# Last super-block: new keys and values turned by VectorE and a way through DRAM, undivided last jobs, and a last row scaled by two engines

## The chip, the cores and the metric

The kernel runs on one core of a Trainium2 chip. The metric is the device time of one execution in microseconds. The core has TensorE (PE in the profile; its weight loads are PEld), VectorE (DVE), ScalarE (ACT), GpSimd (POOL) and SyncE (SP), which issues nearly all DMAs of this kernel. TensorE writes into eight PSUM banks; the other data lies in SBUF or in DRAM.

## The reference

One layer of a streaming encoder. 2048 prompt rows and 64 rows of a running stream, 1024 wide, are normalised and multiplied by one input matrix of 4096 columns. Half of the columns feed attention (8 heads of 64), half a gated linear recurrence (4 heads of 128). Cut to what matters here:

```python
def mixer_layer(x, ln_g, w_in, lb, norm_g, w_out, attn_fn, s0):
    aq, ak, av, ag, hq, hf, hi, hg = jnp.split(rms_norm(x, ln_g) @ w_in, SPLITS, axis=-1)
    k, v = heads(ak), heads(av)
    o_a = attn_fn(heads(aq), k, v).reshape(B, T, W_A) * jax.nn.silu(ag)
    o_b, S = hgrn2_branch(hq, hf, hi, hg, lb, norm_g, s0)
    y = x + jnp.concatenate([o_a, o_b], axis=-1) @ w_out
    return y, k, v, S

# attention: each chunk of 64 frames sees itself and the 8 chunks before it, plus a learned bias
# recurrence, per block of frames (b: running sum of log f, bl: its last value):
S = jnp.exp(bl)[..., None] * S + jnp.einsum('bshk,bshv->bhkv', kb * jnp.exp(bl[:, None] - b), vb)
# outputs: final RMSNorm of y for prompt and sample, the last 512 rows of k and v of the prompt
# and the 64 of the sample, and the recurrent states
```

The rows of k and v that are returned for the prompt are the last 512, which are exactly the rows of the last super-block below. `kb * exp(bl - b)` are the decayed keys.

## The kernel before, in words

**Tiling.** The rows are worked in four super-blocks: rows 0 to 511, rows 512 to 1023 with the 64 sample rows (576), rows 1024 to 1535, rows 1536 to 2047. In each, 32 jobs (`project`) multiply the normalised input, held transposed with features on partitions, by 128 columns of the input matrix. Every float32 operand is split into a high and a low part, so one job is 24 matmuls of 128x128 weights over 512 columns, or over 256 and 320 in the 576-row super-block. Jobs have a kind and a number: `hf hq hi hg` for the heads 0 to 3 of the recurrence, `pg pq pk pv` (gate, query, key, value) for the pairs 0 to 3 of attention heads. The result lands transposed in a PSUM bank `acc` (two of them): features on partitions, rows of the sequence along the free axis.

**After a job.** Each kind has a function that empties the bank (`ev_f`, `ev_k`, ...). Some data must be turned, so that sequence rows lie on partitions:
- values: for the super-blocks 0 to 2, `ev_v` lets DVE transpose 32x32 blocks out of `acc` (`turn_blocks`), sends them to a DRAM room with four DMAs, and fetches them back with one (`turn_rows`), after which whole rows of 128 features stand on the partitions. For the last super-block, `ev_v_last` copies the bank to a tile `vT`, turns it by eight 64x64 TensorE transposes for the product with V, and by four 128x128 ones for the rows to be returned (`new_rows`: transposes into bank `tr`, DVE copy to a tile `sig` at L645, one DMA).
- keys: `ev_k` copies the bank to `vT`, splits it into the key tile `kd`, and in the last super-block `new_rows` turns and returns the rows.
- input values of the recurrence (`ev_i`): the DVE and DRAM way in every super-block.
- decayed keys (`rec_block`): tile `kh` (buffer `bl`), per 128 rows one TensorE transpose into a bank `g` and an ACT copy to `kn` (L1474), which is then the weight operand of the product with the input values.

The silu gates and the forget gates (`silu_to` at L575, `ev_f` at L1248) also pass through `sig`, of which there are two buffers; `vT` has three. `ev_k` copies at L794, `ev_v_last` at L815.

**Jobs in halves.** The second job and the last two of a super-block are run in two halves of 256 columns, so that the two halves of the rows can be taken over one after the other between super-blocks; this includes the last two jobs of the last super-block, `pk` and `pg` of pair 3.

**The end.** The output projection runs as 7 products of 12 matmuls for each of 8 row pairs (`out_step`), added to the residual (`out_add`); POOL adds in two pieces of 256. `out_norm` is called for each half of a row tile (128 rows x 512 columns): ACT squares and sums it; after the second half ACT makes the inverse root, and DVE scales by it and the gain vector `g_in` (L1860), half after half, each with a DMA by SP.

**What sets the order.** The program order of every engine is written out at build time by a planner (`Plan`): generators yield the time from which they can go on, tokens (`tk`) stand for buffers and banks, and `C.dve`, `C.act`, `C.dma` advance a modelled clock of each engine and of SP's queue. On the chip each engine and SP's queue then run strictly in that order, with semaphores between them. TensorE's order interleaves jobs with attention, recurrence and output steps. Weight loads (L446) wait on SP for TensorE to free one of four weight buffers.

Of the kernel before, what the change touches and what calls it, by code (L numbers as in the profile page):

```python
# [8 lines left out]
F32 = mybir.dt.float32  # L9
# [3 lines left out]
ALU = mybir.AluOpType  # L13
# [4 lines left out]
P = 128  # L18
# [165 lines left out]
def hymba_step(  # L184
# [439 lines left out]
    def new_rows(src, off, bn, p, out_p, out_s, tok, t):  # L624
# [29 lines left out]
            tk["sig"].put()  # L654
        tk["tr"].put(1, t)

    def split_rows(src, v, h, t0, nt, rows, t):
        s = src.rearrange("p (h a t j) -> p h a t j", h=2, a=2, t=nt)[:, h]
        hi, lo = (v[:rows, h, t0 : t0 + nt, x, :].rearrange("p t (a j) -> p a t j", a=2) for x in (h, 1 - h))
        act.copy(hi, s)  # L660
        t = C.act(nt * 64 + 80, t)
        yield "D", t
        dve.tensor_sub(lo, s, f32(hi))
        return C.dve(nt * 64 + 30, t)
# [74 lines left out]
    def pair_jobs(sb, p):  # L739
        t0, n = SUPER[sb][:2]  # L740
        last = sb == len(SUPER) - 1
        smp = n > WIN
        d = Pair()
        d.sb, d.p = sb, p
# [45 lines left out]
        def ev_k(acc, off, bn, t):  # L790
            yield from tk["vT"].get()
            yield "A", t
            kn = T(wk, [P, 512], F32, "vT", bufs=VTB)
            act.copy(kn[:, :bn], acc)  # L794
            t = C.act(bn, t)
            tk["acc"].put(1, t)
            c = slice(512 + off, 512 + off + bn)
            for h in range(2):
                yield lambda: d.open[h]
                yield "A", t  # L800
                act.copy(d.kd[own[h], h, c], kn[own[h], :bn])
                t = C.act(bn, t)
                yield "D", t
                dve.tensor_sub(d.kd[own[1 - h], h, c], kn[own[h], :bn], f32(d.kd[own[h], h, c]))
                t = C.dve(1.2 * bn, t)
                d.k_n[h] += bn
                d.k_t[h] = max(d.k_t[h], t)
            yield from new_rows(kn, off, bn, p, nk_prompt if last else None, nk_sample, tk["vT"], t)
            yield from got_all(True)

        def ev_v_last(acc, off, bn, t):
# [28 lines left out]
        def ev_v(acc, off, bn, t):  # L840
            yield from tk["vT"].get()
            yield "D", t
            vt = T(wk, [P, 512], F32, "vT", bufs=VTB)
            t = turn_blocks(vt, acc, bn)
            tk["acc"].put(1, t)
            t = yield from turn_rows(vt, bn, t)
            full = bn // P * P
            parts = [p_ for p_ in ((0, full, P, None),
                                   (full, P if bn > full else 0, bn - full, nv_sample)) if p_[1]]
            for c, w, rows, out in parts:  # L850
                if out is not None:
                    rows_out(vt[:rows, c : c + w], out, slice(p * P, (p + 1) * P), t)
            for h in range(2):
                yield lambda: d.open[h]
                for c, w, rows, _ in parts:
                    yield "A", t
                    t = yield from split_rows(vt[:rows, c : c + w], d.v, h, 4 + (off + c) // P, w // P, rows, t)
                d.v_n[h] += bn
                d.v_t[h] = max(d.v_t[h], t + 500.0)
            tk["vT"].put(1, t)  # L860
            yield from got_all(False)

        def all_in():
# [37 lines left out]
            yield from gate(acc, off, bn, t)  # L901
            d.sg_n += bn

        return d, dict(g=ev_g, q=ev_q, k=ev_k, v=ev_v_last if last else ev_v)

    def softmax_rows(d, h, qc, spans, bcol, nk, out):

# [428 lines left out]
    def rec_block(r, off, bn, lastb):  # L1336
# [10 lines left out]
        def v3(t):  # L1347
            return t[:, :bn].rearrange("p (b t) -> p b t", t=32)
# [86 lines left out]
                              fk[:, :nprc].unsqueeze(3).to_broadcast([P, nprc, 2, 32]), ALU.mult)  # L1435
            td = C.dve(1.9 * bn, td)
        qh, kh = tmp("bm"), tmp("bl")
        dve.tensor_tensor(v3(kh), v3(k1), sf[:, :nb].unsqueeze(2).to_broadcast([P, nb, 32]), ALU.mult)
        tkh = C.dve(1.3 * bn)
        dve.tensor_tensor(v3(qh), v3(q1), pf[:, :nb].unsqueeze(2).to_broadcast([P, nb, 32]), ALU.mult)  # L1440
        tqh = C.dve(1.3 * bn)

# [19 lines left out]
            m = mask[:w, :w].unsqueeze(1).to_broadcast([w, cs.stop - cs.start, w])  # L1462
            dve.copy_predicated(A[:w, cs, :w], m, ag[:w, cs, :w])
        ta = C.dve(1.1 * bn, t)
        yield max(ta, tkh) + 200.0
        tg = bank()
        for i, (cc, nbk, smp) in enumerate(chunks):
            w = nbk * 32
            transpose(tg[:w, i], kh[:, cc : cc + w], ident)
        t = C.pe()  # L1470
        yield "A", t
        kn = tmp("k1").rearrange("p (c t) -> p c t", t=P)
        for cs, w in merged():
            act.copy(kn[:w, cs], tg[:w, cs])  # L1474
        t = C.act(bn, t)
        yield t + 200.0
        kv = bank()
        iv = r.iv
        for i, (cc, nbk, smp) in enumerate(chunks):
# [343 lines left out]
    def out_norm(o, tile_, half, t):  # L1823

        rows = o["rows"]
        x = o["res"][tile_]
        end = o is outp.get(len(pairs) - 1)
        yield "A", t
        yield from tk["ck"].get()
        junk = T(wk, [P, D], mybir.dt.bfloat16, "ck", bufs=1)  # L1830
        ss = T(wk, [P, 1], F32, "ss", bufs=4)
        act.activation(junk[:rows, :512], x[half][:rows], AF.Square, accum_out=ss[:rows])  # L1832
        t = C.act(800, t)
        tk["ck"].put()
        if tile_ not in o["first"]:
            o["first"].add(tile_)
            b0 = T(wk, [P, 1], F32, "b0", bufs=4)
            yield "D", t
            dve.tensor_scalar(b0[:rows], ss[:rows], 1.0 / D, EPS, ALU.mult, ALU.add)
            C.dve(10, t)  # L1840
            o["b0"][tile_] = b0
            return
        yield lambda: tile_ in o["b0"]
        r = T(wk, [P, 1], F32, "rstd", bufs=4)
        act.activation(r[:rows], ss[:rows], AF.Ln, bias=o["b0"][tile_][:rows], scale=1.0 / D)
        act.activation(r[:rows], r[:rows], AF.Exp, scale=-0.5)
        t = C.act(400, t)
        y = o["y"][tile_]
        if x[3] is not None and not end:
            yield "D", t  # L1850
            dve.scalar_tensor_tensor(x[3][:rows], x[3][:rows], r[:rows], g_in[:rows], ALU.mult, ALU.mult)
            t = C.dve(1070, t)
            yield t
            sp.dma_start(y, x[3][:rows])
            C.dma(512 * rows / P)
        else:
            for a in range(2):
                c = slice(a * 512, a * 512 + 512)
                yield "D", t
                dve.scalar_tensor_tensor(x[a][:rows], x[a][:rows], r[:rows], g_in[:rows, c], ALU.mult, ALU.mult)  # L1860
                t = C.dve(530, t)
                yield t
                sp.dma_start(y[:, c], x[a][:rows])
                C.dma(256 * rows / P)
        for tag in x[2]:
            tk[tag].put(1, C.now + 4000.0)
# [46 lines left out]
    def program():  # L1913
# [66 lines left out]
        for sb in range(nsb):  # L1980
            last = sb == nsb - 1
            halves = SUPER[sb][3]
            blocks = SUPER[sb][2]
            if sb == 2:
                C.spawn(out_weights(), 3)
            made = {}
            for u, (kind, g) in enumerate(JOBS[sb]):
                if u == len(JOBS[sb]) - 8:
                    if last:
                        C.spawn(out_load(0), 1.5)  # L1990
                        C.spawn(out_load(1), 1.6)
                        for rows in (out_rows_w(), out_rows_g(), out_rows_x(), out_rows_a()):
                            C.spawn(rows, 2)
                    else:
                        for half in range(2):
                            off, bn = SUPER[sb + 1][3][half]
                            for c in range(off, off + bn, P):
                                C.spawn(x_tile(sb + 1, half, c), 0.5 + 0.1 * half)
                if (kind[0], g) not in made:
                    d, evs = made[kind[0], g] = (head_jobs if kind[0] == "h" else pair_jobs)(sb, g)  # L2000
                    C.spawn((recurrence if kind[0] == "h" else attention)(d), 1)
                evac = made[kind[0], g][1][kind[1]]

                if u in (1, len(JOBS[sb]) - 1):
                    for half in range(2):
                        yield from project(j - 1, [halves[half]], before, half == 1,
                                           lambda part, k0: x_ready(sb, half, part, k0))
                        yield from project(j, [halves[half]], evac, half == 1,
                                           lambda part, k0: x_ready(sb, half, part, k0))
                        if u > 1:  # L2010
                            x_left[sb, half] = True
                elif u not in (0, len(JOBS[sb]) - 2):
                    yield from project(j, blocks, evac)
                before = evac
                j += 1
        for i, k in steps:
# [147 lines left out]
```

## Time and profile before

| what | value |
|---|---|
| median of 3 runs | 1251.13 us (1250.59 to 1251.42) |
| profiled execution | 1251.06 us |
| its span, first to last instruction | 1249.3 us, granted clock 0.998 |
| TensorE busy | 1237.7 us, 7520 matmuls |
| DVE, ACT, POOL busy | 886.6, 684.4, 412.3 us |
| DMA | 287.94 MB in 137956 packets, 230 GB/s |

The span lies within the profiled execution's time; 1.8 us are outside it. A row of TensorE is a matmul from its start to its modelled end, and the next one starts before that end, so lengths of rows don't add up, while the distances from start to start do. The last super-block's jobs run from about 805 to 1065 us; the output steps follow until 1242.7 us, and the last row's work until the end.

### The profile page before, as it was taken

Reading aid. Unit: us, or ns where it says so; the run is one execution under the profiler, and the core shown is the slowest. Engines: PE = TensorE matmul, PEld = TensorE weight load, DVE = VectorE, ACT = ScalarE, POOL = GpSimd, SP = SyncE. Lnnn points to the kernel's source line nnn. Section 1 sums busy time; section 2 is a strip of 40 time slices with the busy share of each in tenths; the row PEclk is TensorE's granted clock in tenths of the full one; section 3 lists DMA queues with packets and bytes.
Section 4 is the critical chain, followed back from the end, with each engine's and each line's share of the span. In section 5 each row is a group of like instructions: output and inputs, shape, how many; then the busy total and the mean of one; then the engine's idle time right before and its main releaser. Section 6 shows DMA issues by size and latency. Waiting matters only on the chain. (4 is left out here: it accounts for less than half of the span.)

```text
span 1249.3 us, 21363 instructions
## 1 busy us (share of the span) xinstructions
PE 1237.7 (99%) x7520; PEld 1088.6 (87%) x7520; DVE 886.6 (71%) x1889; ACT 684.4 (55%) x1534; POOL 412.3 (33%) x702
## 2 busy tenths in 40 slices
PE   9999999999999999999999999999999999999997
PEld 8888888999999999998888888988888888788786
DVE  7697878866767578776576677775757476767775
ACT  6354545665656556574555566664655445643443
POOL 7666564101020111200233242133241103474543
PEclk9999999999999999999999999999999999999999
DMA  8897888666565474654777778687766655887431
GB/s 337 301 325 257 313 301 318 203 192 222 166 195 166 144 276 155 206 178 150 284 247 252 266 263 280 227 258 248 231 243 210 218 203 211 333 273 237 139 123 68
DMA packets 137956, 287.94 MB, mean 230 GB/s; under 512 B 35257, under 2 KB 79289, under 8 KB 120186
## 3 DMA queue, kind: packets, MB, share of 16 engines
q1 hardware_dynamic: 137560, 286.58, 67.6%
q8 instruction: 59, 0.97, 0.3%
q14 instruction: 47, 0.39, 0.1%
q10 hardware_dynamic: 290, 0.01, 0.0%
HBM read 195.31 MB, written 92.27 MB: 230 GB/s over the span
## 5 line engine op out<-in xcount | busy, mean ns | idle before, releaser
L249 PE MATMUL acc<-xh,w 128*128 128x512 f32 (+2 forms) x2752 | 568.6, 345 | 0.5 <-ACT xh L409 0.5
L249 PEld LDWEIGHTS acc<-xh,w 128*128 128x128 f32 x2752 | 439.3, 189 | 50.6 <-ACT xh L409 0.9
L249 PE MATMUL acc<-xl,w 128*128 128x512 f32 (+2 forms) x1376 | 294.8, 345 | 0.0
L249 PEld LDWEIGHTS acc<-xl,w 128*128 128x128 f32 x1376 | 221.1, 189 | 24.4
L939 ACT ACTIVATE pr<-pr,nm 128x640 f32<-128x640 f32 (+4 forms) x132 | 100.4, 761 | 60.0 <-DVE nm L922 59.5
L951 ACT CAST ph<-tr 128x512 fp32r<-128x512 f32 (+3 forms) x176 | 88.2, 507 | 78.5 <-PE pv L249 45.8
L922 DVE CUSTOM_DVE_ANT_0 pr<-s,bias 128x640 f32<-128x640 f32 (+4 forms) x128 | 94.2, 736 | 41.1 <-PE s L249 40.3
L473 POOL TENSOR_TENSOR w<-wraw,w 128x256 fp32r<-128x256 f32 x120 | 102.4, 884 | 55.0 <-DVE w L468 43.1
L954 DVE TENSOR_TENSOR ph<-tr,ph 128x512 fp32r<-128x512 f32 (+3 forms) x176 | 101.2, 588 | 26.3 <-ACT ph L951 25.5
L249 PE MATMUL pv<-ph,v 128*128 128x256 f32 (+2 forms) x344 | 98.6, 370 | 0.1
L253 PE MATMUL tr<-ident,pr 128*128 128x128 f32 x580 | 88.1, 273 | 1.3 <-DVE ph L954 1.3
L993 DVE TENSOR_TENSOR mixa<-mixa,pv 64x256 f32<-64x256 f32 (+1 forms) x144 | 56.9, 395 | 43.3 <-ACT mixa L989 39.7
L510 POOL TENSOR_TENSOR xn<-wraw,xn 128x256 fp32r<-128x256 f32 x48 | 39.0, 814 | 142.4 <-ACT xn L507 137.1
L1095 POOL TENSOR_TENSOR mixa<-mixa,sga 128x256 f32<-128x256 f32 (+1 forms) x36 | 27.9, 776 | 162.8 <-DVE mixa L993 152.0
L253 PEld LDWEIGHTS tr<-ident,pr 128*128 128x128 f32 x580 | 69.7, 140 | 10.9 <-issue 1.7
L943 DVE TENSOR_SCALAR pr<-pr,sm 128x640 f32<-128x640 f32 (+4 forms) x132 | 74.6, 565 | 4.7
L1532 POOL TENSOR_TENSOR k<-ob 128x512 f32<-128x512 f32 (+2 forms) x20 | 18.2, 910 | 176.0 <-ACT ob L1523 136.0
L575 ACT ACTIVATE sig<-acc 128x512 f32<-128x512 f32 (+2 forms) x64 | 32.2, 503 | 74.6 <-PE acc L249 72.0
L249 PEld LDWEIGHTS pv<-ph,v 128*128 128x128 f32 (+1 forms) x344 | 58.2, 189 | 7.3 <-issue 0.5
L989 ACT COPY mixa<-pv 64x256 f32<-64x256 f32 (+1 forms) x72 | 25.2, 350 | 64.8 <-PE pv L249 59.5
L249 PE MATMUL s<-kd,q 128*128 128x320 f32 (+2 forms) x232 | 55.8, 310 | 0.0
L249 PE MATMUL s<-kd,ql 128*128 128x320 f32 (+2 forms) x232 | 55.5, 309 | 0.0
(333 smaller groups left out, 2133.3 us busy)
## 6 DMA issues: line engine op xcount, KB each, us to landing
w<-wd SPq DMA_DIRECT2D x96, 1024.0 KB, 5.8
wd<-w SPq DMA_DIRECT2D x32, 1024.0 KB, 7.3
wraw<-in_w_in_dram SPq DMA_DIRECT2D x30, 512.0 KB, 5.3
wod<-xn SPq DMA_DIRECT2D x28, 512.0 KB, 5.5
xn<-in_x_prompt_dram SPq DMA_DIRECT2D x23, 512.0 KB, 4.6
bias<-biasd SPq DMA_DIRECT2D x24, 320.0 KB, 5.9
carry<-kd SPq DMA_DIRECT2D x12, 512.0 KB, 7.0
carry<-v SPq DMA_DIRECT2D x12, 512.0 KB, 5.5
```

What stands on the lines that cost most here:

```text
L249: pe.matmul(out, w, x, **kw)
L253: pe.transpose(out, x, idn)
L473: pool.tensor_sub(w[:, 1, k : k + 2], raw[:, k : k + 2], f32(w[:, 0, k : k + 2]))
L510: pool.tensor_sub(f32r(st[:, c.start + 512 : c.stop + 512]), src[:, c], st[:, c])
L575: act.activation(sig[:, :bn], acc, AF.Exp, scale=-1.0)
L922: dve.tensor_tensor_reduce(s[:, :nk].rearrange("p (a c) -> p a c", a=ns), sps[:, :ns, :kn], d.bias[:, h, bcol : bcol + nk].rearrange("p (a ...
L939: act.activation(s[:, :nk], s[:, :nk], AF.Exp, bias=nm[:, 0:1], scale=-1.0, accum_out=sm)
L943: dve.tensor_scalar(s[:, :nk], s[:, :nk], sm, None, ALU.mult)
L951: act.copy(ph[:krows, 0, :wid], pt[:krows, :wid])
L954: dve.tensor_sub(ph[:krows, 1, :wid], pt[:krows, :wid], f32(ph[:krows, 0, :wid]))
L993: dve.tensor_add(mix[hs, :qn], mix[hs, :qn], pv[hs, i, :qn])
L1095: pool.tensor_mul(mix[:, :n], mix[:, :n], d.sg[:, g0 : g0 + n])
```

## The change

- Keys of pairs 0 to 2 in the last super-block: the rows to be returned are turned by `turn_blocks` into a `sig` tile and a way through DRAM (`block_rows`), and go out by four DMAs with pieces of 128 bytes (`rows_to`). Pair 3 keeps the transposes.
- Values of the same pairs: `ev_v`, the way of the other super-blocks, takes the place of `ev_v_last`; the rows go out by `rows_to`, and the `vT` tile is kept 4 us longer in the planner's time.
- Decayed keys of heads 0 and 1 in super-blocks 1 to 3: written in the order that the way needs, turned by DVE, sent through DRAM beside the rest of the block, and copied by ACT from SBUF instead of from PSUM.
- The last two jobs of the last super-block run whole, one after the other.
- The last row tile: the half that is finished first is multiplied by the gain on DVE while the other is still summed; at the end ACT scales it and issues its DMA, and DVE scales the other half, which SP sends.

```diff
+    def rows_to(src, out, off, w, p):
+        s4 = src.rearrange("q (a t j) -> q t a j", a=4, j=32)
+        for i in range(w // P):
+            row = off + i * P
+            sp.dma_start(out[row : row + P, p * P : (p + 1) * P].rearrange("q (a j) -> q a j", a=4), s4[:, i])
+            C.dma(64)
+            yield C.now + 800.0
+
+    def block_rows(src, off, bn, p, out, tok, t):
+        yield from tk["sig"].get()
+        yield "D", t
+        st = T(wk, [P, 512], F32, "sig", bufs=2)
+        t = turn_blocks(st, src, bn)
+        tok.put(1, t)
+        t = yield from turn_rows(st, bn, t)
+        yield t
+        yield from rows_to(st[:, :bn], out, off, bn, p)
+        tk["sig"].put(1, C.now + 4000.0)
...
+        by_blocks = last and p < NPAIR - 1
...
+            if by_blocks:
+                yield from block_rows(kn, off, bn, p, nk_prompt, tk["vT"], t)
+            else:
+                yield from new_rows(kn, off, bn, p, nk_prompt if last else None, nk_sample, tk["vT"], t)
...
+                elif by_blocks:
+                    C.spawn(rows_to(vt[:, c : c + w], nv_prompt, off + c, w, p), 2)
...
-            tk["vT"].put(1, t)
+            tk["vT"].put(1, t + (4000.0 if by_blocks else 0.0))
...
-        return d, dict(g=ev_g, q=ev_q, k=ev_k, v=ev_v_last if last else ev_v)
+        return d, dict(g=ev_g, q=ev_q, k=ev_k, v=ev_v_last if last and not by_blocks else ev_v)
...
+        by_dma = sb > 0 and h < 2
...
+                dve.tensor_tensor(kh4, k14, sf[:, : 4 * nprc].rearrange("p (c b) -> p c b", b=4).unsqueeze(3)
+                                  .to_broadcast([P, nprc, 4, 32]), ALU.mult)
...
+                    dve.transpose(kh[:, a_[0] : a_[1]], kh[:, a_[0] : a_[1]])
...
+                rows["t"] = yield from turn_rows(kh, bn, tkh)
...
+            yield lambda: "t" in rows
+            yield rows["t"]
+            kn = tmp("k1").rearrange("p (c t) -> p c t", t=P)
+            if nprc:
+                act.copy(kn[:, :nprc].rearrange("p c (a j) -> p c a j", j=32),
+                         kh[:, :full].rearrange("p (a c j) -> p c a j", a=4, j=32))
...
+            if end and tile_:
+                yield "D", 0.0
+                c = slice(half * 512, half * 512 + 512)
+                dve.tensor_mul(x[half], x[half], g_in[:, c])
+                C.dve(530)
+                o["scaled"] = half
...
+        elif end and tile_:
+            a = o["scaled"]
+            act.mul(x[a], x[a], r)
+            act.dma_start(y[:, a * 512 : a * 512 + 512], x[a])
+            c = slice((1 - a) * 512, (1 - a) * 512 + 512)
+            dve.scalar_tensor_tensor(x[1 - a], x[1 - a], r, g_in[:, c], ALU.mult, ALU.mult)
+            sp.dma_start(y[:, c], x[1 - a])
...
-                if u in (1, len(JOBS[sb]) - 1):
+                if u == 1 or (u == len(JOBS[sb]) - 1 and not last):
...
-                elif u not in (0, len(JOBS[sb]) - 2):
+                elif u != 0 and (last or u != len(JOBS[sb]) - 2):
                     yield from project(j, blocks, evac)
+                    if u == len(JOBS[sb]) - 1:
+                        x_left[sb, 0] = x_left[sb, 1] = True
```

More of the change, by code (lines that the diff above doesn't have):

```diff
@@ L807, in ev_k @@
                 d.k_t[h] = max(d.k_t[h], t)
-            yield from new_rows(kn, off, bn, p, nk_prompt if last else None, nk_sample, tk["vT"], t)
+            if by_blocks:
+                yield from block_rows(kn, off, bn, p, nk_prompt, tk["vT"], t)
+            else:
+                yield from new_rows(kn, off, bn, p, nk_prompt if last else None, nk_sample, tk["vT"], t)
             yield from got_all(True)
@@ L1437, in rec_block, with row_way @@
         qh, kh = tmp("bm"), tmp("bl")
-        dve.tensor_tensor(v3(kh), v3(k1), sf[:, :nb].unsqueeze(2).to_broadcast([P, nb, 32]), ALU.mult)
-        tkh = C.dve(1.3 * bn)
+        by_dma = sb > 0 and h < 2
+        full = nprc * P
+        rows = {}
+        if not by_dma:
+            dve.tensor_tensor(v3(kh), v3(k1), sf[:, :nb].unsqueeze(2).to_broadcast([P, nb, 32]), ALU.mult)
+            tkh = C.dve(1.3 * bn)
+        else:
+            if nprc:
+                k14, kh4 = (a_[:, :full].rearrange(o_, b=4, j=32) for a_, o_ in
+                            ((k1, "p (c b j) -> p c b j"), (kh, "p (b c j) -> p c b j")))
+                dve.tensor_tensor(kh4, k14, sf[:, : 4 * nprc].rearrange("p (c b) -> p c b", b=4).unsqueeze(3)
+                                  .to_broadcast([P, nprc, 4, 32]), ALU.mult)
+            if bn > full:
+                k13, kh3 = (a_[:, full:bn].rearrange("p (b j) -> p b j", j=32) for a_ in (k1, kh))
+                dve.tensor_tensor(kh3, k13, sf[:, 4 * nprc : nb].unsqueeze(2).to_broadcast([P, nb - 4 * nprc, 32]),
+                                  ALU.mult)
+            C.dve(1.3 * bn)
+            for a_ in ((0, full), (full, bn)):
+                if a_[0] < a_[1]:
+                    dve.transpose(kh[:, a_[0] : a_[1]], kh[:, a_[0] : a_[1]])
+            tkh = C.dve(1.1 * bn)
+            def row_way():
+                rows["t"] = yield from turn_rows(kh, bn, tkh)
+            C.spawn(row_way(), 1)
         dve.tensor_tensor(v3(qh), v3(q1), pf[:, :nb].unsqueeze(2).to_broadcast([P, nb, 32]), ALU.mult)
@@ L1464, in rec_block @@
         ta = C.dve(1.1 * bn, t)
[L1465 to L1476, printed above, removed]
+        kn = None
+        if by_dma:
+            yield ta + 200.0
+            yield lambda: "t" in rows
+            yield rows["t"]
+            kn = tmp("k1").rearrange("p (c t) -> p c t", t=P)
+            if nprc:
+                act.copy(kn[:, :nprc].rearrange("p c (a j) -> p c a j", j=32),
+                         kh[:, :full].rearrange("p (a c j) -> p c a j", a=4, j=32))
+            if bn > full:
+                act.copy(kn[:DEC, nprc], kh[:DEC, full : full + P])
+            t = C.act(bn, rows["t"])
+            yield t + 200.0
+        else:
+            yield max(ta, tkh) + 200.0
+            tg = bank()
+            for i, (cc, nbk, smp) in enumerate(chunks):
+                w = nbk * 32
+                transpose(tg[:w, i], kh[:, cc : cc + w], ident)
+            t = C.pe()
+            yield "A", t
+            kn = tmp("k1").rearrange("p (c t) -> p c t", t=P)
+            for cs, w in merged():
+                act.copy(kn[:w, cs], tg[:w, cs])
+            t = C.act(bn, t)
+            yield t + 200.0
         kv = bank()
```

## The prediction

> **What bounds the kernel now.** I read the page first for busy shares, then the list of what TensorE waits for, then TensorE in order of time around the instructions that go, and last the end of the chain.
>
> ```profile
> span 1249.3 us, 21363 instructions
> PE 1237.7 (99%) x7520; PEld 1088.6 (87%) x7520; DVE 886.6 (71%) x1889; ACT 684.4 (55%) x1534; POOL 412.3 (33%) x702
> ...
> PE tr L253 <- DVE ph L954: 1.3, 1, 1.3
> PE acc L249 <- DVE pr L1783: 0.6, 1, 0.6
> ```
>
> TensorE is busy 99% of the span, and its longest wait after the start is 1.3 us. Busy alone could hide waits, because a matmul's row lasts longer than the time to the next one, so I use the distance between starts:
>
> ```profile
> 863.39 1.99 PE L249 MATMUL acc<-xh,w 128*128 128x512 f32 x8
> 865.22 0.60 PE L253 MATMUL tr<-ident,vT 128*128 128x128 f32 x4
> 865.58 0.70 PE L249 MATMUL acc<-xh,w 128*128 128x512 f32 x2
> 866.12 0.45 PE L249 MATMUL s<-kd,q 128*128 128x320 f32 x2
> ...
> 867.25 0.46 PE L253 MATMUL tr<-ident,vT 64*128 64x64 f32 x4
> 867.65 1.20 PE L249 MATMUL acc<-xh,w 128*128 128x512 f32 x4
> 868.68 0.62 PE L249 MATMUL acc<-xl,w 128*128 128x512 f32 x2
> ...
> 912.06 0.60 PE L253 MATMUL g<-ident,bl 128*128 128x128 f32 x4
> 912.41 0.72 PE L249 MATMUL acc<-xl,w 128*128 128x512 f32 x2
> 912.97 0.62 PE L249 MATMUL pv<-ph,v 128*128 128x512 f32 x2
> ```
>
> Columns: start, length, engine, line, tiles, shape, count. Eight 512-wide matmuls take 863.39 to 865.22, 0.229 us each, with no hole when the transposes come between. So TensorE is a full queue: the time is the sum of what it is given, plus the last row after it. An instruction taken off it is worth its distance to the next start, if what it made still comes in time from elsewhere.
>
> **Transposes taken off TensorE.** A group's price is from its start to the second row behind it, less the matmuls between at 0.229, because a group's last transpose shows its cost only in the matmul behind it.
> - Four 128x128 transposes for output rows: 866.12 - 865.22 - 2 x 0.229 = 0.44 us. Keys and values of pairs 0 to 2: 6 groups, 2.6 us.
> - Four 64x64 transposes that bring one head's values into place: 868.68 - 867.25 - 4 x 0.229 = 0.51 us. Two heads, three pairs: 6 groups, 3.1 us.
> - Decayed keys: 912.97 - 912.06 - 2 x 0.229 = 0.45 us for four, 0.112 each.
>
> ```profile
> L253 PE MATMUL g<-ident,bl 128*128 128x128 f32 x64 | 10.2, 272 | 0.0
> ...
> L253 PE MATMUL g<-ident,bl 128*64 128x128 f32 x4 | 1.1, 272 | 0.0
> ```
>
> 64 and 4 are those of four heads, so 17 a head. A head has four of the wide ones in super-block 0, where nothing changes; 13 stay to be removed for each of heads 0 and 1: 26 x 0.112 = 2.9 us. The three together: 8.6 us.
>
> **What takes their place.** On DVE the rows of keys were a copy of 512 columns from PSUM and become a 32x32-block transpose of 512; the values' row copy likewise gives way to one block transpose; only the decayed keys gain an instruction, eight of at most 0.71 us, some 6 us over 950 us. ACT loses three copies of values (L815).
>
> ```profile
> L671 DVE STREAM_TRANSPOSE vT<-acc 128x512 f32<-128x512 f32 x18 | 12.8, 711 | 5.3 <-PE acc L249 5.2
> ...
> L645 DVE COPY sig<-tr 128x512 f32<-128x512 f32 x7 | 4.8, 690 | 3.7 <-PE tr L253 3.7
> ...
> 900.00:950.00 50.00, 50.00 (x292) 42.27 (x292) 31.67 (x65) 28.17 (x59) 18.27 (x26) 1.00 0.72 249
> ```
>
> In that stretch of the last super-block DVE is busy 31.7 of 50 us, so it covers this at no cost; without the cover it would be at most those 6 us. The clock granted is 1.00 and DMA engines are busy 0.72, also with room.
>
> SP's queue gets more. A way is four DMAs out and one back; rows are four DMAs instead of one. Keys or values of a pair: +8, six times 48; heads 0 and 1: five parts a head (1, 2, 1, 1 over the blocks), five DMAs each, +50. At 0.43 us an issue 98 DMAs are 42 us, 24 us of them (58 DMAs) in the last super-block.
>
> ```profile
> SPq L446 <- PE acc L249: 94.5, 23, 12.0
> ...
> SPq L695 <- DMA way<-vT: 9.2, 5, 5.6
> ...
> L691 SPq DMA_DIRECT2D way<-vT x184: 302/430/1898, 32.4 to 1011.0; - x184
> ...
> way<-vT SPq DMA_DIRECT2D x72, 64.0 KB, 5.0
> vT<-way SPq DMA_DIRECT2D x18, 256.0 KB, 5.6
> ```
>
> The first two rows are SP's waits between 800 and 1060 us: 94.5 us in 23 waits for TensorE to free a weight buffer (L446). Issues go into that time. What queues behind a way's return wait (5.6 us at most there) is chiefly the weight loads, which run up to three jobs ahead, 24 x 0.229 = 5.5 us of TensorE each. With SP's slack gone, 24 us would be the most it costs; I take nothing.
>
> Latency: a way is 0.71 (DVE) + 4 x 0.43 + 5.0 + 0.34 + 5.6 = 13 us. For the decayed keys it runs beside the input values' own way, issued at about the same time, and both must be in before the products; in super-block 1's second block it lies bare, but there TensorE has projections to run. For values of pair 0:
>
> ```profile
> 865.42 0.59 ACT L815 COPY vT<-acc 128x512 f32<-128x512 f32 x1 [1.38 <-PE acc L249]
> ...
> 870.28 0.46 PE L253 MATMUL tr<-ident,vT 64*128 64x64 f32 x4
> ```
>
> The copy starts at 865.42 and the second head's transposes at 870.28, so the values are in place near 871.5; by the way they are there near 865.4 + 13 + 1 = 879.5, 8 us later, and pair 1 the same. TensorE goes on with the next head's jobs meanwhile. Pair 2's values come two whole jobs ahead of its keys. I take zero, the bound below is the gain of the 1.3 us wait shown above (its PSUM bank is one that the row transposes also use), the bound above is in the rivals.
>
> **Last two jobs whole.** 96 matmuls of 256 become 48 of 512.
>
> ```profile
> 1051.46 1.11 PE L249 MATMUL acc<-xl,w 128*128 128x256 f32 x8
> 1052.41 1.36 PE L249 MATMUL acc<-xh,w 128*128 128x256 f32 x10
> ```
>
> Eight take 0.95 us, 0.119 each: 96 x 0.119 - 48 x 0.229 = 0.4 us less. The keys of pair 3 end half a pair of jobs earlier; the normalised input has long been in place there, so nothing needs the halves.
>
> The Trainium skill ("TensorE: Matmul & The Clock Gate", Part 1, "Wait — 56ns, not 53.3ns?") puts a warm matmul at its columns over 2.4 GHz plus about 2.5 ns, 109 and 216 ns here, by which this part would give 0.1 us instead. The trace has 119 and 229, more by 10 and 13, so I keep the trace's.
>
> **The last row.**
>
> ```profile
> 1240.56 0.15 DVE L1839 TENSOR_SCALAR b<-ss 128x1 f32<-128x1 f32 x1
> 1242.76 0.69 DVE L1783 TENSOR_TENSOR pr<-pr,acc 128x512 f32<-128x512 f32 x1 [2.05 <-issue]
> 1243.36 1.41 DVE L1860 SCALAR_TENSOR_TENSOR bias<-bias,rstd,gin 128x512 f32<-128x512 f32 x2
> 1244.80 1.41 DVE L1860 SCALAR_TENSOR_TENSOR pr<-pr,rstd,gin 128x512 f32<-128x512 f32 x2
> ...
> 1244.56 0.20 ACT L1846 ACTIVATE rstd<-rstd 128x1 f32<-128x1 f32 x1
> ...
> 1245.61 0.96 SPq L1863 DMA_DIRECT2D out_dram<-pr  x2
> ...
> out_dram<-xn SPq DMA_DIRECT2D x8, 512.0 KB, 2.6
> ...
> out_dram<-pr SPq DMA_DIRECT2D x6, 256.0 KB, 2.1
> ```
>
> Now DVE scales both halves after ACT's 1244.76, and SP issues the second DMA some 0.6 us after the first (two issues in 0.96). After, the early half's product with the gain (0.69) fits DVE's 2.05 us of idleness before 1242.76; then ACT scales one half while DVE does the other, and two queues issue at about 1245.5. At most one DVE step goes, 0.62 us. But the transfers then overlap: 512 KB land in 2.6 us, 256 KB in 2.1, which takes back 0.5. The ends are 0.1 and 0.62; should the product land behind 1242.76 instead, the end comes 0.1 to 0.6 later than now. I take 0.3 us gained.
>
> **Sum.** 8.6 + 0.4 + 0.3 = 9.3 us. The profiled execution took 1251.06 us, 1.8 over its span; the median of the runs is 1251.13. 1251.1 - 9.3 = 1241.8.
>
> **Rivals.**
> - *The data comes late and TensorE waits* (partly lost). Values of pairs 0 and 1, 8 us later, hold up the products with V, these the release of the pair's key and value room, and this the next pair's loads. If a third of the delay is not filled, at V and at the next pair's keys of pair 0 and at V of pair 1, 3 x 2.7 = 8 us of the gain goes, half of that in a mild case: 1246 to 1250. Against: the same way serves all values of super-blocks 0 to 2 and all input values, and TensorE's waits show nothing of them.
> - *A buffer is held too long* (slower). The rows of keys keep one of two "sig" buffers through the way and the row DMAs.
>
> ```profile
> 858.88 0.59 ACT L794 COPY vT<-acc 128x512 f32<-128x512 f32 x1 [1.19 <-PE acc L249]
> ...
> 875.57 0.59 ACT L1248 ACTIVATE sig<-acc 128x512 f32<-128x512 f32 x1
> ...
> 883.92 0.60 ACT L575 ACTIVATE sig<-acc 128x512 f32<-128x512 f32 x1 [1.26 <-PE acc L249]
> ...
> DMA to landing us min/median/max: 1.8/1.8/2.1
> ```
>
>   The last row is for 32 KB written in 128-byte pieces (L621); a row DMA is 64 KB of them, 3.6 us as an estimate from it. Pair 0: 859.5 + 13 + 2 (issues) + 3.6 = 878, while the first silu job takes the other buffer at 875.57 and the next one needs the first at 883.92. Margin 6 us, and one more job of 5.5 us fits the second accumulator before TensorE stops. It decides only if rows land 11.5 us late; at 17 us late, three pairs lose 3 x 5.5 = 16.5, that is 1258. The Trainium skill ("DMA: Bandwidth & Descriptors", Specifications) says that transfers below 512 B are done as read-modify-write and do not reach line rate, which would push this way; the trace's 1.8 us for 128-byte pieces does not show it.
> - *Nothing changes.* The removed transposes only filled time in which TensorE would have waited for DVE or DMA anyway: 1249 to 1251. Against: TensorE's distances between starts are the same with and without transposes between them.
>
> **How the numbers follow.** Forecast 0.74, its own range 1239.8 (the 1.3 us wait and 0.62 at the end gained too) to 1243.8 (2 us of new waits); late data 0.15; nothing changes 0.05; buffer held 0.06. About 0.2%, 2.5 us, is what a measurement of this kernel can tell from no change: faster is below 1248.6. The forecast and two thirds of the late-data cases are faster with some to spare: 0.87; same 0.08; slower 0.05. The range 1239.8 to 1247 leaves out the slow cases and half of late data.
>
> **What would show it.** Right: 74 fewer matmul rows from transposes and 48 fewer from the last jobs, 7398 in all; TensorE's waits still a few us in all; busy time lower by about what the span loses; the two output DMAs at the end on two queues less than 0.3 us apart. Wrong: new waits of TensorE for V, the key and value loads or the accumulator, several us each, behind pair 0 or 1; ACT or DVE waiting for row DMAs; SP waits for "way" far over 5.6 us with weight loads behind them.

## The result, and the profile after

The changed kernel takes 1255.12 us (median; 1254.78 to 1256.72) against 1250.86 (1250.44 to 1251.42) for the kernel before on the same chip: ratio 1.0037, 95% interval 1.0026 to 1.0047. It is 4.3 us slower, where 9.3 us less were forecast, and lies above the forecast's range of 1239.8 to 1247. The profiled execution, from which the rows come, took 1256.72, 1.6 over the median.

The busy line from the page of the changed kernel, and TensorE's three longest waits (total, times, longest):

```profile
span 1255.0 us, 21260 instructions
PE 1231.5 (98%) x7398; PEld 1080.1 (86%) x7398; DVE 897.8 (72%) x1897; ACT 680.4 (54%) x1526; POOL 417.1 (33%) x702
...
PE acc L249 <- DVE sga L580: 8.1, 1, 8.1
PE pv L2038 <- POOL one L279: 1.4, 1, 1.4
PE acc L249 <- DMA v<-wod: 1.3, 1, 1.3
```

The matmuls are the 7398 that were forecast, and TensorE's busy time fell by 6.2 us. But there is one wait of 8.1 us that the kernel before doesn't have. TensorE waits for DVE's gate product (L580). DVE's own longest wait between 1050 and 1080 us is the first line below (the next longest is 1.8), and the chain that ended last goes through the same transfer (second line: start, length):

```profile
DVE sig L645 <- DMA out_dram<-sig: 9.1, 1, 9.1
```

```profile
1057.72 9.68 DMA out_dram<-sig
```

In order of time, all engines:

```profile
1056.15 0.94 SPq L2102 DMA_DIRECT2D w<-wod  x2
...
1057.00 0.69 DVE L645 COPY sig<-tr 128x512 f32<-128x512 f32 x1
...
1057.61 0.81 DVE L947 CUSTOM_DVE_ANT_0 pr<-s,bias 128x640 f32<-128x640 f32 x1
...
1057.72 10.90 SPq L650 DMA_DIRECT2D out_dram<-sig  x2
...
1060.37 0.39 PE L249 MATMUL acc<-b11l,slot 128*128 128x512 f32 x1
...
1067.51 0.69 DVE L645 COPY sig<-tr 128x512 f32<-128x512 f32 x1 [9.09 <-DMA out_dram<-sig]
1068.12 0.68 DVE L580 TENSOR_TENSOR sga<-acc,sig 128x512 f32<-128x512 f32 x1
...
1068.86 2.07 PE L249 MATMUL acc<-w,slot 128*128 128x512 f32 x4 [8.10 <-DVE sga L580]
```

This is pair 3, which keeps the TensorE transposes. Its first row copy (1057.00) fills a `sig` buffer, whose DMA is issued at 1057.72. One softmax step later (L947, done by 1058.4) DVE's order has the second row copy into the same buffer, because the gate (`silu_to`) holds the other one; it must wait until the transfer has read the buffer, and starts at 1067.51. Behind it in DVE's order stands the gate product, which empties an `acc` bank. TensorE's next product goes into that bank, so TensorE stops.

The stop and what follows it, in windows (length, then busy time of TensorE, its weight loads, DVE, ACT and POOL, the granted clock, DMA share, GB/s), first after, then before:

```profile
1060.00:1068.80 8.80, 0.76 (x4) 0.29 (x2) 1.29 (x3) 0.58 (x1) 1.40 (x2) 0.76 0.70 278
1068.80:1074.50 5.70, 5.64 (x15) 4.68 (x16) 3.43 (x10) 1.84 (x4) 0.00 (x0) 0.50 0.78 220
1074.50:1080.00 5.50, 5.50 (x33) 4.77 (x32) 4.11 (x10) 3.72 (x9) 0.63 (x1) 0.96 0.97 385
```

```profile
1060.00:1069.00 9.00, 9.00 (x65) 8.46 (x64) 6.16 (x18) 5.28 (x12) 2.07 (x3) 1.00 1.02 367
1069.00:1074.50 5.50, 5.50 (x30) 4.35 (x29) 5.02 (x14) 3.13 (x8) 0.00 (x0) 1.00 0.75 284
```

After the stop TensorE works 5.7 us at half clock, another 2.9 us lost (half of 5.7): 8.1 + 2.9 = 11.0 in this place, as an estimate. Busy share shows none of the second part, since slow matmuls count as busy.

The end of the execution, after:

```profile
1246.66 0.39 PE L249 MATMUL acc<-v,slot 128*128 128x512 f32 x1
...
1247.74 0.75 DVE L1936 SCALAR_TENSOR_TENSOR bias<-bias,rstd,gin 128x512 f32<-128x512 f32 x1
...
1249.18 0.75 DVE L1930 SCALAR_TENSOR_TENSOR pr<-pr,rstd,gin 128x512 f32<-128x512 f32 x1 [0.69 <-ACT rstd L1915]
1249.85 0.75 DVE L1936 SCALAR_TENSOR_TENSOR bias<-bias,rstd,gin 128x512 f32<-128x512 f32 x1
...
1250.42 1.27 SPq L1939 DMA_DIRECT2D out_dram<-bias  x2
```

The last half that DVE scales (1249.85) belongs to the row tile before the last (`bias`), and so do the last DMAs. From the end of the last matmul to the end of the span are 1255.0 - 1247.05 = 7.95 us; before, with its last matmul's start at 1242.28 and length 0.39, 1249.3 - 1242.67 = 6.63: 1.3 us more.

By the forecast's own terms: -8.6 - 0.4 for the work, +11.0 and +1.3 make +3.3. The spans differ by 5.7, the medians by 4.3; one to two and a half us lie in small waits.

### The profile page after: what moved, and what is told of

Read it like the earlier page. It is cut to its first block, busy times and chain, and to the rows that moved or that the text cites. A ratio compares the mean times of both kernels' runs of the same rounds, so it can differ in the third digit from the quotient of the medians.

```text
span 1255.0 us, 21260 instructions
## 1 busy us (share of the span) xinstructions
PE 1231.5 (98%) x7398; PEld 1080.1 (86%) x7398; DVE 897.8 (72%) x1897; ACT 680.4 (54%) x1526; POOL 417.1 (33%) x702
## 4 chain that ended last, share of the span: by engine, by line
PE 83%; DVE 5%; DMA 4%; POOL 3%; issue 2%; ACT 2%; SPq 1%; DVEq 0%; ACTq 0%; POOLq 0%
PE acc L249 58%; PE g L249 8%; PE pv L249 6%; PE tr L253 6%; PE s L249 5%; DMA way<-vT 1%; DMA out_dram<-sig 1%; DMA vT<-way 1%; DMA xn<-in_x_prompt_dram 1%; POOL sig L1776 1%; DVE slot L1758 1%; PE g L253 1%; POOL xn L1851 1%; DMA w<-wd 0%; DVE xn L1846 0%
## 5 line engine op out<-in xcount | busy, mean ns | idle before, releaser
L249 PE MATMUL acc<-xl,w 128*128 128x512 f32 (+2 forms) x1360 | 291.4, 346 | 0.8 <-DVE xl L415 0.8
L947 DVE CUSTOM_DVE_ANT_0 pr<-s,bias 128x640 f32<-128x640 f32 (+4 forms) x128 | 94.2, 736 | 55.2 <-PE s L249 54.8
L253 PEld LDWEIGHTS tr<-ident,pr 128*128 128x128 f32 x580 | 69.8, 140 | 10.1 <-DVE ph L979 0.9
```

Source lines behind the costliest of these rows:

```text
L249: pe.matmul(out, w, x, **kw)
L253: pe.transpose(out, x, idn)
L947: dve.tensor_tensor_reduce(s[:, :nk].rearrange("p (a c) -> p a c", a=ns), sps[:, :ns, :kn], d.bias[:, h, bcol : bcol + nk].rearrange("p (a ...
```

## The experiments

Theories named in the expectations: **A**, pair 3's second row copy waits on DVE for the transfer that still reads its buffer, with the gate behind it; **B**, the new ways crowd the DMA queues; **C** and **D**, two readings of what the whole jobs alone do, worded where they are used; **E**, the order of DVE's last scalings costs the time at the end. Numbers are medians, with the ratio to the kernel before on the same chip and its 95% interval. The ratio is not exactly that of the medians; differences in us between two changed kernels compare what each takes off, or adds to, the median of the kernel before on its own chip. Kernels 1 to 4 stand against 1251.27 us, 5 to 8 against 1250.89, 9 to 12 against 1250.92.

**1. The changed kernel with the last two jobs in halves again.**

```diff
-                if u == 1 or (u == len(JOBS[sb]) - 1 and not last):
+                if u in (1, len(JOBS[sb]) - 1):
...
```

> The changed kernel with its last two jobs in halves again. Theory A (a row copy of pair 3 on DVE waits for the DMA that still reads the same sig buffer, and the gate's product stands behind it): the two 512-wide row copies become pieces that come apart in time, the wait of 9.1 us shrinks to at most 3, the half clock after it goes; 1244 to 1248 us. Theory B (the added ways and row DMAs crowd the DMA engines, so that the rows land late whatever the jobs' form): a wait of 5 us or more stays, 1250 us or more.

1248.58 us, 0.9976 [0.9966, 0.9985]: faster than before, though 0.6 us over A's range. The loss needs the whole jobs; the ways without them still gain. Pair 3's row DMAs (L650) land in 2.5 to 2.6 us here, so the new ways alone do not make the rows late, as B would have it.

**2. The kernel before with only the last two jobs whole.** The opposite edit of `project`'s conditions in the old kernel.

> The kernel before with only the last two jobs made whole. Theory A: the wait hangs on how close the two row copies come; here DVE's order has 64 instructions between them, so no wait of DVE for the row DMA, and the part's own 0.4 us is gained: 1250.4 us. If whole jobs alone bring the wait: 1257 to 1262. Theory B: no ways, no wait: 1250.4 as well.

1271.62 us, 1.0161 [1.0146, 1.0176]: by far the slowest, 20 us over the kernel before. None of the expected times came true. DVE, then SP's queue, then TensorE's longest wait after 1060 us:

```profile
1062.99 0.68 DVE L645 COPY sig<-tr 128x512 f32<-128x512 f32 x1
...
1114.51 0.68 DVE L645 COPY sig<-tr 128x512 f32<-128x512 f32 x1
...
1115.70 0.68 DVE L580 TENSOR_TENSOR sga<-acc,sig 128x512 f32<-128x512 f32 x1
```

```profile
1064.14 2.35 SPq L1642 DMA_DIRECT2D sig<-mixd  x2
```

```profile
PE acc L249 <- DMA ph<-wod: 5.9, 1, 5.9
```

Here the loads for the output stage took both `sig` buffers at 1064.14, ahead of pair 3's second row copy and gate. These came 50 us later, and until then one `tr` bank and one `acc` bank stayed full. TensorE's waits between 1060 and 1130 us sum to 14.4 us, against 1.9 in the kernel before. The granted clock (0.80 over 1070 to 1080 us, 0.93 to 1100, 0.62 over 1130 to 1140) adds some 6 us of slow matmuls, as an estimate from busy time. So whole jobs bring the row copies and the gate of pair 3 together, and what then happens hangs on who gets `sig` next: in this kernel the output stage, in the changed one the second copy.

**3. The changed kernel; the buffer is given back 9 us later in the planner's time, about when the transfer lands.**

```diff
-            tk["sig"].put()
+            tk["sig"].put(1, C.now + 9000.0)
```

> The changed kernel, where the planner holds a sig buffer for 9 us after a row DMA's issue, so that DVE's order has the gate's product ahead of the second row copy. Theory A: TensorE's wait of 8.1 us for the gate goes, with the 2.9 us of half clock behind it; what stands behind the copy on DVE may still cost 0 to 4: 1244 to 1248 us. Theory B: rows land as late, and TensorE then waits elsewhere: 1251 us or more.

1246.94 us, 0.9966 [0.9953, 0.9979]: 8.6 us better than the change, by one line that alters only the planned order. DVE:

```profile
1056.58 0.69 DVE L645 COPY sig<-tr 128x512 f32<-128x512 f32 x1
...
1058.26 0.69 DVE L580 TENSOR_TENSOR sga<-acc,sig 128x512 f32<-128x512 f32 x1 [0.25 <-ACT sig L577]
...
1059.04 0.69 DVE L645 COPY sig<-tr 128x512 f32<-128x512 f32 x1
```

The gate now goes first and frees its own `sig` buffer, which the second copy takes without a wait. The first row's transfer is no faster. From issue to landing, the row DMAs (L650) that start between 1055 and 1062 us take, first in the kernel before, then in the changed one, then in this one:

```profile
DMA to landing us min/median/max: 5.9/6.0/6.0
```

```profile
DMA to landing us min/median/max: 9.7/9.7/9.7
```

```profile
DMA to landing us min/median/max: 7.9/8.8/9.7
```

In this kernel the first row lands in 9.7 us and the second in 7.9. The late landing costs nothing when nobody stands behind it. That speaks for A and against B.

The stop was 11.0 us, the kernel gained 8.6. Part of the rest shows as small waits in the same stretch, with the clock at 1.00 (same columns as above):

```profile
1068.80:1074.50 5.70, 5.09 (x31) 3.91 (x29) 4.22 (x11) 3.59 (x9) 1.42 (x2) 1.00 1.05 293
1074.50:1080.00 5.50, 4.80 (x24) 3.43 (x25) 5.43 (x13) 4.21 (x10) 4.95 (x6) 1.00 0.99 411
```

TensorE is idle 1.3 us of these 11.2, where the kernel before has none.

**4. The changed kernel; pair 3's rows of keys in a buffer that is idle at that time.**

```diff
-            yield from tk["sig"].get()
+            yield from tk[room_].get()
...
-            tk["sig"].put()
+            tk[room_].put()
...
+                                    "ck" if last else "sig")
```

(`room_` is a new argument of `new_rows`, "sig" unless given; the values' rows still use `sig`.)

> The changed kernel, where the rows of pair 3's keys use the idle ck buffer instead of sig, so that the second copy needs no buffer that a DMA still reads; order and DMAs stay the same. Theory A: DVE's wait of 9.1 us and TensorE's of 8.1 go, and the half clock: 8.1 + 2.9 = 11 us less than the changed kernel, 1244 us. Theory B: TensorE's waits in this stretch stay 5 us or more, 1250 us or more.

1247.2 us, 0.9967 [0.9954, 0.9979], the same as kernel 3 by another route, and 3 us over A's 1244: here the second copy stays ahead of the gate on DVE, but the first one went into another buffer. So the wait for the shared buffer is the cause of the stop, and the order of kernel 3 is one way to avoid it. Here too the transfers landed late (9.5/9.8/10.1 us), with nobody waiting.

**5. Kernel 2, with the output stage held back until pair 3's gate and key rows are done.**

```diff
-            if last and p == NPAIR - 1 and d.v_n[1] == d.k_n[1] == d.q_n[1] == n:
+            if last and p == NPAIR - 1 and d.v_n[1] == d.k_n[1] == d.q_n[1] == d.sg_n == d.rows_n == n:
                 have.add("projected")
...
```

> The kernel before with the last two jobs whole, where the loads of the output stage take the sig and vT buffers only after pair 3's gate and both row copies are done. Theory C (alone, whole jobs were slow because the output stage took both sig buffers first, so that pair 3's row copy and gate came 50 us late, kept a tr and an acc bank, and pair 3's attention and the last output weights fell back by 20 us): those waits go, at most 3 us of a wait for the row DMA stay; 1250 to 1254 us. Rival D (whole jobs are slow of themselves, since the keys and the gate come out in blocks of 512 at one time): 1260 us or more.

1252.2 us, 1.0012 [1.0003, 1.0021]. The 20 us of kernel 2 are gone (C, not D), so they came from the order around `sig`. What is left is no gain but a loss of 0.4 to 2.6 us: the 0.4 us of shorter matmuls don't show.

**6. The kernel before with only the new last row.**

> The kernel before with only the new last row. Theory E (the second half of the row tile before it is now scaled behind the last one on DVE, so that its DMA is issued last and four transfers of 256 KB fall together): about 1.3 us more from the last matmul to the end, 1252.4 us. The prediction's step: 0.3 us less, 1250.8.

1251.91 us, 1.0007 [0.9999, 1.0016]. The interval allows nothing to 2 us more, but not the forecast's 0.3 us less; the trace has the sequence of the changed kernel, the second scaling of the early tile after the last tile's:

```profile
1245.42 0.75 DVE L1867 SCALAR_TENSOR_TENSOR pr<-pr,rstd,gin 128x512 f32<-128x512 f32 x1 [0.69 <-ACT rstd L1852]
1246.09 0.75 DVE L1873 SCALAR_TENSOR_TENSOR bias<-bias,rstd,gin 128x512 f32<-128x512 f32 x1
1246.66 1.27 SPq L1876 DMA_DIRECT2D out_dram<-bias  x2
```

From the end of its last matmul (1243.30) to the end of its span (1251.3) are 8.0 us, against 6.63 before.

**7. Only keys and values of pairs 0 to 2 by the new way** (`by_dma = False`, jobs in halves, old last row), and **8. only the decayed keys** (`by_blocks = False`, the same).

> The kernel before with only the ways of keys and values of pairs 0 to 2. The prediction's price (6 groups at 0.44, 6 at 0.51): 5.7 us less, 1245.4 us, with no new wait of TensorE before 1045 us. Theory B (late data and crowded DMAs take it back): 1248 us or more, with waits for V or for loads in the last super-block.

> The kernel before with only the decayed keys of heads 0 and 1 by DVE and DRAM. The prediction's price (26 transposes at 0.112): 2.9 us less, 1248.2 us. Theory B: the ways of the recurrence come late and TensorE waits in super-blocks 1 to 3: 1250 us or more.

Kernel 7: 1246.31 us, 0.9961 [0.9947, 0.9974], that is -4.6 us with an interval from -6.6 to -3.3. Kernel 8: 1248.76 us, 0.9983 [0.9974, 0.9992], -2.1 us from -3.3 to -1.0. The forecast had -5.7 and -2.9; both lie inside, on the side of the larger gain. The busy lines have 48 and 26 matmuls less than the 7520 of before:

```profile
PE 1232.8 (99%) x7472; PEld 1084.8 (87%) x7472; DVE 888.0 (71%) x1889; ACT 681.1 (55%) x1531; POOL 413.3 (33%) x702
```

```profile
PE 1234.5 (99%) x7494; PEld 1085.6 (87%) x7494; DVE 893.1 (72%) x1901; ACT 683.0 (55%) x1534; POOL 412.3 (33%) x702
```

**9. Kernel 4 with the hold of kernel 5, and the last row put in order:** DVE's second scaling of the tile before the last is issued directly behind its first.

```diff
-                yield "D", t
+                if not (end and a):
+                    yield "D", t
...
                 t = C.dve(530, t)
-                yield t
+                if not end:
+                    yield t
```

> The changed kernel with the keys' rows in the ck buffer, the output loads held until pair 3's gate and rows are done, and in the last row both halves of the tile before it scaled and sent ahead of the last ones. Theory A: e4's time (1247.2 us) less what the order on DVE cost at the end, 1.3, and less the 0.1 to 0.6 of the prediction's step: 1245.5 us. If the transfers at the end and not the order took the 1.3: no change to e4, 1247 us.

1245.68 us, 0.996 [0.9948, 0.9973], 5.2 us under before where kernel 4 was 4.1 under, with overlapping intervals: the hold and the order together add little to the separate buffer, and nothing that goes beyond kernel 12 below.

**10. Both ways, jobs in halves, old last row,** and **11. the same with the new last row in order** (kernel 1 with the edit above).

> The kernel before with both sets of ways (pairs 0 to 2, heads 0 and 1), jobs in halves and the old last row. If the parts add up: 4.6 + 2.1 less, 1244.2 us. If they take from each other in the stretch from 1045 to 1080 us, as the waits of e1 there show (5.3 us in all): 1247.3 us, e1 less the last row's 1.2.

> e1 (both ways, halves, new last row) with both halves of the tile before scaled and sent ahead of the last ones. Theory E: the 1.3 us at the end go and 0.1 to 0.6 are gained: e1's 1248.6 less 1.6, 1247.0 us; beside e10 it is 0.1 to 0.6 faster. If overlapping transfers took it: the same as e1.

Kernel 10: 1247.39 us, 0.9971 [0.996, 0.9982], -3.5 us. The two ways together gain less than their gains alone, 4.6 + 2.1 = 6.7, would make: the interval of kernel 10 is -5.0 to -2.3. Its longest waits of TensorE:

```profile
PE acc L249 <- ACT vT L814: 2.4, 1, 2.4
PE tr L253 <- DVE v L855: 1.2, 1, 1.2
```

They lie at about 1055 to 1058 us, in pair 3's halves; in the same stretch kernel 7 has 0.4 us of the first and kernel 8 neither. Kernels 1 and 11, also with both ways and halves, have both waits too (1.8 or 1.6, and 1.2). They are about as large as the missing 3.2 us. Behind the first stands an ACT copy that waited for DVE (L802) to finish reading a `vT` buffer:

```profile
1056.24 0.37 ACT L814 COPY vT<-acc 128x256 f32<-128x256 f32 x1 [0.93 <-DVE ql L802]
```

What delays it with both ways was not tested. Kernel 11: 1246.76 us, 0.9973 [0.9965, 0.9982], 0.6 us under kernel 10, with intervals that overlap.

**12. Kernel 3 with the last row in order.**

> e3 (the changed kernel, a sig buffer held 9 us in the planner after a row DMA) with the last row's order mended as in e9: e3's 1246.9 less 1.6, 1245.3 us.

1244.28 us, 0.9956 [0.9942, 0.997]: 6.6 us faster than before, 10.9 faster than the change. It is the shortest time of all, but the intervals of kernels 7 and 9 overlap its own. Its end:

```profile
1236.45 1.41 DVE L1937 SCALAR_TENSOR_TENSOR bias<-bias,rstd,gin 128x512 f32<-128x512 f32 x2
...
1237.89 0.75 DVE L1930 SCALAR_TENSOR_TENSOR pr<-pr,rstd,gin 128x512 f32<-128x512 f32 x1
...
1238.64 0.37 ACTq L1928 DMA_DIRECT2D out_dram<-pr  x1
1238.70 0.33 SPq L1931 DMA_DIRECT2D out_dram<-pr  x1
```

Both halves of the early tile are done before the last tile's scale is known, and the last two DMAs leave within 0.06 us of each other, as the change meant it. The last matmul ends at 1235.76, the span at 1242.4: 6.6 us, no longer 7.95 and as long as before. In whole times the row's order shows less clearly: between kernels 1 and 11, 4 and 9, 3 and 12 the ratio falls by 0.0003, 0.0007 and 0.0010, all within the intervals. But the same stretch can be read off every trace: with the new row as the change has it (the changed kernel and kernels 1, 3, 4, 6) it is 7.9 to 8.0 us, with the new row in order (9, 11, 12) 6.6, and with the old row (the kernel before and kernels 2, 5, 7, 8, 10) 6.5 to 6.8. So E holds, at 1.1 to 1.5 us.

## Why the prediction was wrong, step by step

- **Transposes taken off TensorE (8.6 us): right for each part alone, not reached together.** The counts are exact, and each part measured alone has its price in its interval. Adding the parts was not borne out: both ways gave 3.5 us with the jobs in halves (kernel 10, at most 5.0 by its interval) and 6.6 at best (kernel 12, at most 7.3).
- **What takes their place (nothing): right behind pairs 0 to 2, as far as the waits show.** In the changed kernel TensorE shows no wait of several us for values, key loads or a way there; kernel 10's 2.4 and 1.2 us lie in pair 3. SP's slack was used as foreseen: between 800 and 1060 us its waits for weight buffers fall from 94.5 us to

```profile
SPq L446 <- PE acc L249: 29.0, 14, 6.1
...
SPq L661 <- DMA vT<-way: 19.2, 3, 7.8
```

  and waits for the ways, up to 7.8 us, take part of their place without a stop of TensorE. The rows in 128-byte pieces were estimated at 3.6 us; the typical one (L661) landed in 1.9:

```profile
DMA to landing us min/median/max: 1.8/1.9/6.0
```

  The Trainium skill ("DMA: Bandwidth & Descriptors", Specifications) warns of read-modify-write below 512 B. At 64 KB a transfer, this trace shows no such price in the time to landing, but no run has the same rows in larger pieces beside it.
- **Last two jobs whole (-0.4 us): the step that failed.** It priced the matmuls and looked at the input: "the normalised input has long been in place there, so nothing needs the halves". It didn't look at the output side. The halves also staggered pair 3's row copies and its gate over time, and with them the claims on two `sig` buffers. Whole, they come at once: +11.0 us at the stop in the changed kernel, +20 us alone, and no gain without the ways even with the order repaired (kernel 5). In whole times the step cost 7.0 us, from kernel 1 (-2.7) to the changed kernel (+4.3): halves beside the ways have the waits of kernel 10, which whole jobs do not. With the order repaired, whole jobs beside the ways stand 1.6 and 2.5 us better than halves (kernel 3 against 1, 12 against 11), with intervals that overlap. Whole jobs beside the ways also moved a transfer: two 1 MB output-weight loads (1056.15) now precede the row DMA (1057.72), where before it was the other way round:

```profile
1061.11 0.94 SPq L650 DMA_DIRECT2D out_dram<-sig  x2
...
1063.25 2.00 SPq L2024 DMA_DIRECT2D w<-wod  x2
```

  6.0 us to landing became 9.7, and 9.5 to 10.1 in kernel 4, where the same loads also go first. Why the loads come earlier was not traced.
- **The last row (-0.3 us): wrong sign, +1.3 in the trace.** The working followed the last tile alone. The new branch hands over no time between its instructions, while the branch of the tile before the last does so between its two halves; so the new branch's scaling was written into DVE's order ahead of that tile's second half, whose DMAs then ended the kernel. In the right order nothing is gained or lost that can be seen at the end (6.6 us, as before), so the forecast's 0.3 us are not there either.
- **Rivals.** "A buffer is held too long" named the right buffer and the right kind of stop, but at pair 0 and through the new ways, with a margin of 11.5 us. The real place was pair 3, which the change leaves on its old path: there the buffer was given back too early in the planner's time. The rival of late data was not seen behind pairs 0 and 1.
- **Small sums.** Three of the forecast's sums don't come out: 58 DMAs at 0.43 us are 25 us, not 24; 0.74 and two thirds of 0.15 are 0.84, not 0.87; and the range's lower end, with 1.3 us more and 0.62 in place of 0.3 gained, is 1240.2, not 1239.8. None of them bears on the step that failed.

**What stays open:** why the two ways together gain 3.2 us less than apart while the jobs are in halves, and the 2.5 us between kernel 12 and the forecast. In kernel 12 all waits are short (1.5 us in four is the largest group), and unchanged parts of the program differ by about 1 us from one profile to another: the same score matmuls start at 301.75 us in the kernel before and at 302.79 in kernel 6, which differ only in the last row.

## What to carry to other kernels

When a planner writes each engine's order, a buffer must come back in its model when the transfer out of it has landed, not when it is issued: here that one line was worth 8.6 us, since it put the gate ahead of the copy that would have waited. Price a wait by everything that stands behind it on an in-order engine, and for a step that brings work together in time, list the buffers and banks that its outputs claim, also for the parts that are "not changed". A branch that hands over no time between its instructions overtakes those that do, so the end of a kernel has to be read for every tile that is still under way, not for the last one alone.

## What the hardware showed that was not expected

One stop of 8.1 us cost 2.9 us more through the clock: 0.50 granted for 5.7 us of full work behind it (the rows 1068.80 to 1074.50 above). In narrower windows the clock is 1.00 up to 1064.5 us and 0.66 from there to 1065.0, then 0.50, then 0.60 from 1074.5 to 1075.0 and 1.00 again. So it fell to half at about 1064.7, some 3.9 us into the stop, and came back at about 1074.9, some 6.0 us into the work: 10.2 us at half. The Trainium skill ("TensorE: Matmul & The Clock Gate", Part 1, "What's actually happening") has half clock after at least one idle window of about 3.4 us, and full clock after at least one window of about 3.4 us of sustained work, in windows that run freely and do not start with the work. The trace agrees: 10.2 us are three such windows, of which the work filled only the last from end to end, so the return could take more than 3.4 us.

A row DMA of 256 KB landed 9.7 us after its issue when two 1 MB loads had been issued 1.6 us before it, against 6.0 us without loads ahead of it. In kernels 1, 10 and 11, where the loads come some 8 us behind the first row DMA, it landed in 2.6, and in kernel 7 two row DMAs ahead of the loads landed in 2.5 and 2.7 while one of 128 KB issued 2.6 us behind them took 6.9. That the loads are the cause is argued from this order; it was not tested by moving them, and the 6.0 us of the kernel before, with its loads behind, show that they are not all.
